# Issuing the stores of a SwiGLU kernel from GpSimd, and one gate and one product per tile in place of two

## The chip, the cores and the metric

One core of one Trainium2 chip. The metric is the time of one execution on the device in microseconds (us). The kernel before takes 936.15 us (median of 3 runs, 936.01 to 936.37). A profile records one execution; its span is some 2 us shorter than the timed run. In the views ACT is ScalarE (the gates), DVE is VectorE (the products), POOL is GpSimd and SP is SyncE; a name with q is that engine's queue of instructions. A store or load is *issued* when its engine starts it and has *landed* when its last byte is in place; a *packet* is the piece that one of the 16 DMA engines moves at a time, here a row of 64 KB (load) or 32 KB (store).

## The reference

```python
x = np.random.randn(8192, 8192).astype(np.float32)
a, b = np.split(x, 2, axis=-1)
silu_b = b / (1 + np.exp(-b))
return a * silu_b          # 8192 x 4096 float32
```

268.4 MB are read and 134.2 MB are written, with one gate and one product per output element.

## The kernel before

Two rows of x are one partition's share of a tile: 128 partitions x 16384 floats (64 KB), 32 tiles, three tile buffers. Each row is `a` (4096) and then `b` (4096). The gate works in place on `b`; the product goes to the front of the tile, from where the store takes it.

```python
R = 2; BUFS = 3                     # ntiles = 32, last = 31
def load(i, rows=None):  ...        # nc.sync.dma_start; whole tile, or one row of each pair
def swiglu(i, k, c0=0, cw=half):
    b = xt[:, k * M + half + c0 : k * M + half + c0 + cw]
    nc.scalar.activation(out=b, in_=b, func=_SILU)
    nc.vector.tensor_mul(out=xt[:, k * half + c0 : ...], in0=xt[:, k * M + c0 : ...], in1=b)
def store(i, c0=0, cw=R * half):
    (nc.scalar if i < last - 1 else nc.sync).dma_start(...)

nc.vector.memset(zt, 0.0)
nc.scalar.dma_start(out=ov[0:P, 0:128], in_=zt)     # the early zero store
for i in range(BUFS): load(i)
for i in range(last):
    for k in range(R): swiglu(i, k)
    if i == last - 1: swiglu(last, 0)
    store(i)
    ...                             # load(i + 3); the last tile in two row loads
store(last, 0, half)
...                                 # second row of the last tile in two halves, then its store
```

A load into a buffer must wait until the store of that buffer has landed. This ties everything into a ring: load, gate and product, store, next load, with three buffers going round.

Of the kernel before, what the change touches and what calls it, by code (L numbers as in the profile page):

```python
# [1 line left out]

# [4 lines left out]

_SILU = mybir.ActivationFunctionType.Silu


@with_exitstack
def kernel(
    ctx: ExitStack,
    tc: tile.TileContext,
    x: bass.AP,
    out: bass.AP,
):




    nc = tc.nc
    N, M = x.shape
    half = M // 2
    P = nc.NUM_PARTITIONS
    R = 2
    BUFS = 3

    xv = x.tensor.reshape([N // R, R * M]).ap()  # L30
    ov = out.tensor.reshape([N // R, R * half]).ap()
    ntiles = N // (P * R)
    last = ntiles - 1

    pool = ctx.enter_context(tc.tile_pool(name="sbuf", bufs=BUFS))
    tiles = {}

    def load(i, rows=None):
        if i not in tiles:
            tiles[i] = pool.tile([P, R * M], x.dtype, name="xt")  # L40
        lo, hi = (0, R) if rows is None else rows
        nc.sync.dma_start(  # L42
            out=tiles[i][:, lo * M : hi * M], in_=xv[i * P : (i + 1) * P, lo * M : hi * M]
        )

    def swiglu(i, k, c0=0, cw=half):
        xt = tiles[i]
        b = xt[:, k * M + half + c0 : k * M + half + c0 + cw]
        nc.scalar.activation(out=b, in_=b, func=_SILU)  # L49
        nc.vector.tensor_mul(  # L50
            out=xt[:, k * half + c0 : k * half + c0 + cw],
            in0=xt[:, k * M + c0 : k * M + c0 + cw],
            in1=b,
        )

    def store(i, c0=0, cw=R * half):
        (nc.scalar if i < last - 1 else nc.sync).dma_start(
            out=ov[i * P : (i + 1) * P, c0 : c0 + cw], in_=tiles[i][:, c0 : c0 + cw]
        )


    zt = ctx.enter_context(tc.tile_pool(name="zeros", bufs=1)).tile([P, 128], x.dtype, name="zt")
    ctx.enter_context(tc.manual_schedule())
    nc.vector.memset(zt, 0.0)  # L64
    nc.scalar.dma_start(out=ov[0:P, 0:128], in_=zt)

    for i in range(BUFS):
        load(i)
    for i in range(last):
        for k in range(R):  # L70
            swiglu(i, k)
        if i == last - 1:
            swiglu(last, 0)
        store(i)
        nxt = i + BUFS
        if nxt < last:
            load(nxt)
        elif nxt == last:
            load(last, (0, 1))
            load(last, (1, 2))  # L80

    store(last, 0, half)
    for c0 in range(0, half, half // 2):
        swiglu(last, 1, c0, half // 2)
    store(last, half, half)


# [1 line left out]
_INS = ['x']  # L89
_OUTS = [((8192, 4096), 'float32')]  # L90


# [23 lines left out]
```

## Time and profile before

| what | before |
|---|---|
| median time | 936.15 us |
| span of the profile | 933.9 us |
| DMA engines busy, both queues | 99.8% |
| DVE, ACT busy | 30%, 25% |
| one turn of a buffer (3 tiles) | 87.1 us |
| of it landing to store issue | 12.6 us |

First the view of DMA issues (queue, count, KB, median time from issue to landing):

```profile
out_dram<-xt ACTq DMA_DIRECT2D x30, 4096.0 KB, 40.0
...
xt<-in_x_dram SPq DMA_DIRECT2D x31, 34.2
```

A store needs 40.0 us and a load 34.2 us from issue to landing, though one tile of each passes every 29.0 us. The excess is time spent queued behind the transfer before. Then the view of windows over the middle of the span (length; busy time of DVE, ACT, POOL; clock; DMA share; GB/s):

```profile
100.00:883.00 783.00, 238.97 (x54) 192.30 (x54) 0.00 (x0) 1.00 1.00 434
```

DMA share 1.00 and 434 GB/s: the 16 engines never pause here.

### The profile page before, as it was taken

To read this page: it belongs to the slowest core of one execution; us is meant where nothing else is said; L and a number is where in the kernel's file an instruction comes from. 1 tells how busy PE (TensorE), PEld (TensorE's weight loads), DVE (VectorE), ACT (ScalarE), POOL (GpSimd) and SP (SyncE) were. 2 spreads that over 40 slices of the span, in tenths; PEclk is the share of its full clock that TensorE was granted. 3 is DMA by queue.
4 is the path that set the end of the run, shared out by engine and by line. 5 is a ranking of instruction groups with operands and counts; after the bars stand their busy time and mean duration, and the time that the engine had idled before them with its cause. 6 is when DMAs were issued, how large, how long until landed. Compare 5 with 4: busy or idle time off the path is not lost.

```text
span 933.9 us, 370 instructions
## 1 busy us (share of the span) xinstructions
DVE 283.5 (30%) x66; ACT 229.4 (25%) x66; POOL 0.2 (0%) x4
## 2 busy tenths in 40 slices
DVE  0333312333113332133321333213332133331252
ACT  0323330233312333113331133311333203332041
POOL 0000000000000000000000000000000000000000
DMA  9999999999999999999999999999999999999998
GB/s 407 422 413 460 411 431 441 449 427 420 456 408 445 431 431 441 435 422 441 448 414 436 435 451 425 429 443 414 446 427 436 436 432 425 439 451 411 441 434 383
DMA packets 9650, 402.74 MB, mean 431 GB/s; under 512 B 1072, under 2 KB 1200, under 8 KB 1200
## 3 DMA queue, kind: packets, MB, share of 16 engines
q1 hardware_dynamic: 5184, 276.83, 68.6%
q10 hardware_dynamic: 4464, 125.90, 31.2%
q14 instruction: 2, 0.02, 0.0%
HBM read 268.44 MB, written 134.28 MB: 431 GB/s over the span
## 4 chain that ended last, share of the span: by engine, by line
DMA 84%; DVE 10%; ACT 4%; DVEq 0%; issue 0%; SPq 0%; ACTq 0%
DMA out_dram<-xt 43%; DMA xt<-in_x_dram 41%; DVE xt L50 10%; ACT xt L49 4%; DVEq L111 0%; SPq L42 0%; ACTq L49 0%; DVEq L50 0%
## 5 line engine op out<-in xcount | busy, mean ns | idle before, releaser
L50 DVE TENSOR_TENSOR xt<-xt 128x4096 f32<-128x4096 f32 (+1 forms) x65 | 283.3, 4360 | 635.8 <-ACT xt L49 632.6
L49 ACT ACTIVATE xt<-xt 128x4096 f32<-128x4096 f32 (+1 forms) x65 | 228.1, 3556 | 686.5 <-DMA xt<-in_x_dram 686.5
L49 ACT ACT_TABLE_LOAD x1 | 1.3, 1283 | 1.5 <-DVE zt L64 1.5
L64 DVE MEMSET zt<- 128x128 f32 x1 | 0.2, 165 | 0.8 <-PEq L100 0.8
L100 POOL MEMSET const-bfloat16-1.0<- 128x1 bf16 x1 | 0.1, 101 | 0.0
L100 POOL MEMSET const-uint8-127<- 128x1 uint8 x1 | 0.1, 101 | 0.0
L100 POOL MEMSET const-float32-0.0<- 128x1 f32 x1 | 0.1, 98 | 0.2 <-issue 0.2
L100 POOL MEMSET const-float32-1.0<- 128x1 f32 x1 | 0.1, 98 | 0.0
## 6 DMA issues: line engine op xcount, KB each, us to landing
out_dram<-xt ACTq DMA_DIRECT2D x30, 4096.0 KB, 40.0
xt<-in_x_dram SPq DMA_DIRECT2D x2, 4096.0 KB, 26.8
out_dram<-xt SPq DMA_DIRECT2D x1, 4096.0 KB, 23.6
out_dram<-xt SPq DMA_DIRECT2D x2, 2048.0 KB, 14.5
xt<-in_x_dram SPq DMA_DIRECT2D x31, 34.2
out_dram<-zt ACTq DMA_DIRECT2D x1, 64.0 KB, 24.1
```

Of the source, the lines that this page charges most:

```text
L49: nc.scalar.activation(out=b, in_=b, func=_SILU)
L50: nc.vector.tensor_mul(out=xt[:, k * half + c0 : k * half + c0 + cw], in0=xt[:, k * M + c0 : k * M + c0 + cw], in1=b,)
L64: nc.vector.memset(zt, 0.0)
L100: nc = _bacc.Bacc("TRN2", target_bir_lowering=False, num_devices=1)
```

## The change

The intent: ACT should do only gates, GpSimd (otherwise idle) should issue the stores, and the fixed cost of half of the compute instructions should go.

```diff
+    def swiglu_tile(i):
+        rows = tiles[i].rearrange("p (k s c) -> p k s c", k=R, s=2)
+        b = rows[:, :, 1, :]
+        nc.scalar.activation(out=b, in_=b, func=_SILU)
+        nc.vector.tensor_mul(
+            out=tiles[i][:, : R * half].rearrange("p (k c) -> p k c", k=R),
+            in0=rows[:, :, 0, :], in1=b)
     def store(i, c0=0, cw=R * half):
-        (nc.scalar if i < last - 1 else nc.sync).dma_start(
+        (nc.gpsimd if i < last - 1 else nc.sync).dma_start(
     ...
     for i in range(last):
-        for k in range(R):
-            swiglu(i, k)
+        if i < BUFS:
+            for k in range(R):
+                swiglu(i, k)
+        else:
+            swiglu_tile(i)
```

More of the change, by code (lines that the diff above doesn't have):

```diff
@@ L54, in swiglu @@
         )
+    def swiglu_tile(i):
[4 more added lines that the diff above has]
+            out=tiles[i][:, : R * half].rearrange("p (k c) -> p k c", k=R),
+            in0=rows[:, :, 0, :],
+            in1=b,
+        )
     def store(i, c0=0, cw=R * half):
-        (nc.scalar if i < last - 1 else nc.sync).dma_start(
+        (nc.gpsimd if i < last - 1 else nc.sync).dma_start(
             out=ov[i * P : (i + 1) * P, c0 : c0 + cw], in_=tiles[i][:, c0 : c0 + cw]
```

## The prediction

> **What bounds the kernel now.** I read the page first (busy shares, the row of DMA shares, the queues), then the chain that ended last in order of time, then the groups of instructions by shape, the waits of the SP queue, and last the single packet records of the trace.
>
> ```profile
> span 933.9 us, 370 instructions
> DVE 283.5 (30%) x66; ACT 229.4 (25%) x66; POOL 0.2 (0%) x4
> ...
> DMA packets 9650, 402.74 MB, mean 431 GB/s; under 512 B 1072, under 2 KB 1200, under 8 KB 1200
> q1 hardware_dynamic: 5184, 276.83, 68.6%
> q10 hardware_dynamic: 4464, 125.90, 31.2%
> ```
>
> The two queues (q1 is SP with the loads and the last three stores, q10 is ACT with the other stores) add up to 99.8% of the time of all 16 DMA engines. No compute engine passes 30%. So the kernel is bound by the bytes that pass the DMA engines, loads and stores together.
>
> The packet records say how tight this is. A 64 KB load row takes 2418 ns, a 32 KB store row 1213 ns, a 16 KB row 611 ns, a 512 B row of the zero store 27 ns. These four lie on one line: about 8.5 ns a packet plus 27.2 bytes per ns. Each engine carries 8 of a tile's 128 rows, so a tile costs an engine 8 x 2418 + 8 x 1213 = 29.05 us. The windows view gives 434 GB/s in every full stretch between 100 and 883 us, and the chain shows the tiles at that same pace:
>
> ```profile
> 393.85 3.63 ACT xt L49
> 397.50 4.44 DVE xt L50
> 402.03 4.44 DVE xt L50
> 406.48 40.22 DMA out_dram<-xt
> 446.78 34.35 DMA xt<-in_x_dram
> 481.20 3.62 ACT xt L49
> ```
>
> The columns are start, length, work. From one gate (393.85) to the gate that ends one turn of the same buffer (481.20) it is 87.35 us, three tiles at 29.1 us. One turn of a buffer is load 34.4, gate and products 12.6, store 40.2. With one tile of each kind passing every 29.05 us, a load that takes 34.4 has queued about 5 us behind the load before it, and a store of 40.2 about 11 us behind the store before it. **Slack in the turn:** 87.1 - 12.6 - 2 x 29.05 = 16.4 us. So long as the compute part of the turn grows by less than this, neither queue need run empty.
>
> What is lost outside this: 32 tiles x 29.05 = 929.5 us is the floor of the packets. The first load packet starts at 1.98 us, the last data packet ends at 932.9 of 933.9. What could still be won is 933.9 - 929.5 - 2.0 - 1.0, some 1.4 us. A gain of 2% would need 917 us, below the floor of the bytes.
>
> **What the Trainium skill says.** (1) "DMA: Bandwidth & Descriptors", section "Issuing engines are not separate DMA queues": DMAs from scalar, sync or gpsimd run on the same 16 engines, and issuing from several saves only sequencer time. The trace agrees as far as it goes: two queues already share the 16 engines to 99.8%. (2) The same page, "Queues, rings and completion order": an engine takes its queues in turn, a packet of each. The trace agrees: the zero store has only 8 small packets per engine, yet lands after 24.1 us, which is about 9 turns, each behind a load packet of 2.418 us (21.8 us, and the start). (3) The same page, "SWDGE vs HWDGE vs iDMA": for a DMA from GpSimd, software on that engine writes the descriptors into rings in SBUF, and a packet is given as at most 4096 B "preferably". No GpSimd DMA is in the kernel before, so the trace can say nothing; this is the main unknown here. (4) "SBUF — State Buffer", section "SBUF: two separate sides": a 2-port DVE operation keeps GpSimd from writing descriptors, while a two-input operation conflicts only with a GpSimd operation that reads SBUF. Here DVE runs only two-input products and one memset at 0.8 us, so I expect no such stall; no trace shows it yet.
>
> **The change part by part.**
>
> ```profile
> L50 DVE TENSOR_TENSOR xt<-xt 128x4096 f32<-128x4096 f32 x63 | 278.8, 4425 | 632.3 <-ACT xt L49 629.1
> L49 ACT ACTIVATE xt<-xt 128x4096 f32<-128x4096 f32 x63 | 224.4, 3608 | 680.5 <-DMA xt<-in_x_dram 680.5
> L50 DVE TENSOR_TENSOR xt<-xt 128x2048 f32<-128x2048 f32 x2 | 4.5, 2288 | 3.5 <-ACT xt L49 3.5
> L49 ACT ACTIVATE xt<-xt 128x2048 f32<-128x2048 f32 x2 | 3.7, 1901 | 6.0 <-DMA xt<-in_x_dram 6.0
> ```
>
> After the bar: busy us in total, mean ns, idle before. Two lengths of each give a line. ACT: (3608 - 1901) / 2048 = 0.834 ns an element, 194 ns fixed; 8192 elements: 7.02 us. DVE: (4425 - 2288) / 2048 = 1.043 ns, 151 ns fixed; 8192: 8.70 us.
>
> *One gate and one product for tiles 3 to 30.* 28 tiles x 2 instructions fall to 28 each; 56 instructions fewer in all. ACT busy falls by 28 x 0.194 = 5.4 us, DVE by 28 x 0.151 = 4.2 us. None of it is on the path, as both idle before every tile for about 20 us. What gets longer is the time from landing to product: before, gate of row 0, then two products, 12.6 us; after, 7.02 + 8.70 + 0.03 = 15.75 us, because the product no longer overlaps the second gate. **Plus 3.15 us per tile**, taken from the 16.4 us of slack.
>
> *Stores from GpSimd, 30 of 32 tiles.* ACT loses 30 issues of 0.34 us and its wait for the product, worth nothing as its next gate is 20 us off. GpSimd has to make 128 rows' descriptors for each. I have no duration of that in this trace; what matters is that 16.4 - 3.15 = 13 us would have to be used up before the DMA could run out of work. It comes right after a product, when DVE next works some 13 us later. Bytes and rows stay; if rows remain packets of 32 KB, the DMA time is 0 different. In turn the loads and stores keep sharing 2 to 1.
>
> *First tiles and end.* Tiles 0 to 2 are by rows as before. The first store has to go through a queue that was not used yet, since the zero store stays on ACT: in the trace of before, the first real store, issued at 35.40, had its first packet at about 39.98, with load packets slowed to 3.3 us around it. A late first store costs nothing while the loads of tiles 1 and 2 (to 74.5) are in the queue. At the end:
>
> ```profile
> 890.75 8.95 DVE L50 TENSOR_TENSOR xt<-xt 128x4096 f32<-128x4096 f32 x2 [20.02 <-ACT xt L49]
> 899.73 20.74 SPq L57 DMA_DIRECT2D out_dram<-xt  x3
> 904.04 3.62 ACT L49 ACTIVATE xt<-xt 128x4096 f32<-128x4096 f32 x1 [9.81 <-DMA xt<-in_x_dram]
> 907.69 4.42 DVE L50 TENSOR_TENSOR xt<-xt 128x4096 f32<-128x4096 f32 x1 [7.99 <-ACT xt L49]
> 913.67 3.71 ACT L49 ACTIVATE xt<-xt 128x2048 f32<-128x2048 f32 x2 [6.02 <-DMA xt<-in_x_dram]
> ```
>
> Tile 30's store is on SP behind the loads of tile 31, which land at 904.0 and 913.67. Its issue moves from 899.7 to about 902.9, still 11 us before its turn. DVE is free at 902.9, before row 0's product at 907.69. After 913.67 the SP queue still has 4.19 + 2.10 + 2.10 MB of stores, 19.3 us at 434 GB/s, far longer than the last half row's compute of 6.4 us. So the end is set by bytes and is not moved. Sum: 0 from compute, 0 from the loop, and I allow +0.5 us for the extra queue's start and end: **936.6 us**.
>
> **The rivals.** (A) *Smaller packets.* If software descriptors cut a 32 KB row into 4 KB, each engine gets 2048 store packets in place of 256; 1792 x 8.5 ns = 15 us, so 951 us (+1.6%). At 2 KB it is 3840 x 8.5 = 33 us, 969 us (+3.5%). Also each piece would wait for a 64 KB load in turn, so that stores crawl until the loads dry up. For it: the skill's preferred packet. Against it: the same trace moves 64 KB rows as single packets from SP and ACT, and the page gives the 4096 B as a preference. I give it 7%, half of that past 2%. (B) *A wait that replaces one.* If a GpSimd store becomes visible late, by over 13 us a tile, the load queue runs empty between a store's landing and the next load; each microsecond beyond it costs up to a third of one per tile, as three buffers share a turn: 5 us too much would be 5/3 x 28 = 47 us. Against it: 128 rows are few. 2%. (C) *One of the 16 engines is slowed* by the fetching of descriptors, and every tile waits for it: 50 ns on each of 256 store packets is 13 us, 949 us. Against it: two descriptors of some bytes beside 32 KB. 4%. (D) *Gain from an ACT that no longer waits, and fewer instructions.* ACT waits 686.5 us for loads, so nothing is gained; at best part of the 1.4 us of loss comes back: 934.7 us.
>
> **Range and chances.** The main case (some 87%) is 935 to 939, with runs of before within 0.4 us. A cost of a new queue of a few us at start or end, and part of A and C, set the upper end: 934.8 to 941. Faster by 2% is excluded by the floor of bytes: 0.01. Slower by 2% (over 954.9) needs A at 2 KB or less, B, or a strong C: 0.05. Same: 0.94.
>
> **What would show it.** Right: a software queue with about 3840 packets of 32 KB, none added under 8 KB beyond the semaphores; DMA share 9 in all slices, 434 GB/s from 100 to 883; ACT x28 at 7.02 us, DVE x28 at 8.70 us; load plus store in one turn down by some 3 to 5 us, to about 70, with the turn still 87. Wrong: many more packets, slices at 8 or less, a period over 29.1 us, or a stretch of more than 1 us at an end without packets.

## The result, and the profile after

| | before | after |
|---|---|---|
| median (6 runs each, range) | 935.98 (935.76 to 936.37) | 936.66 (936.42 to 937.12) |
| ratio | | 1.0007, 95% interval 0.9994 to 1.002 |

A ratio here is the mean time of one kernel's runs over that of the other's in the same rounds, so it is not quite the ratio of the medians quoted. All runs in this document are at clock 1.00. The six runs of each do not overlap, so some 0.7 us are likely to be real, far under 2%.

The page of the kernel after:

```profile
span 934.7 us, 319 instructions
DVE 279.0 (30%) x38; ACT 226.8 (24%) x38; POOL 16.3 (2%) x34
...
DMA packets 9652, 402.76 MB, mean 431 GB/s; under 512 B 1072, under 2 KB 1200, under 8 KB 1200
q1 hardware_dynamic: 5184, 276.83, 68.5%
q0 software_dynamic: 4320, 125.83, 31.2%
q10 hardware_dynamic: 144, 0.07, 0.0%
```

The store bytes moved from q10 to a new queue q0 of kind software_dynamic. Of its 4320 packets 480 are semaphores (30 stores x 16 engines) and 3840 are rows; the lower counts of small packets are the same as before, so a row is still one packet. The packet records give 1213 ns on average, as on ACT's queue (2 of the 3840 took over 1250).

The chain of the kernel after, at the same place as in the prediction (start, length, work):

```profile
394.00 7.04 ACT xt L60
401.06 8.70 DVE xt L61
409.76 0.28 issue
410.05 36.75 DMA out_dram<-xt
446.80 0.02 SPq L42
446.85 34.03 DMA xt<-in_x_dram
480.99 7.04 ACT xt L60
```

From landing to store issue it is now 16.05 us (394.00 to 410.05) in place of 12.63. The store lands after 36.75 us in place of 40.22. The load is unchanged, and the turn is 87.0 us again: **the 3.4 us that compute took longer came wholly out of the time that stores spend queued**. The view of DMA issues and the same window say so for all tiles:

```profile
out_dram<-xt POOLq DMA_DIRECT2D x30, 4096.0 KB, 36.7
...
xt<-in_x_dram SPq DMA_DIRECT2D x31, 34.0
```
```profile
100.00:883.00 783.00, 234.70 (x27) 189.79 (x27) 14.35 (x27) 1.00 1.00 434
```

The groups of the kernel after (count, busy us, mean ns, idle before):

```profile
L61 DVE TENSOR_TENSOR xt<-xt 128x8192 f32<-128x8192 f32 x28 | 243.4, 8693 | 573.4 <-ACT xt L60 573.4
L60 ACT ACTIVATE xt<-xt 128x8192 f32<-128x8192 f32 x28 | 196.8, 7029 | 616.7 <-DMA xt<-in_x_dram 616.7
...
L68 POOL DMA_DIRECT2D out_dram<-xt x30 | 16.1, 536 | 858.5 <-DVE xt L61 773.8
```

7029 and 8693 ns against 7.02 and 8.70 us predicted. A store costs GpSimd 0.53 us, after 0.28 us from the product's end; on ACT the issue took 0.34 us.

The end of the kernel after, by the timeline:

```profile
894.20 8.69 DVE L61 TENSOR_TENSOR xt<-xt 128x8192 f32<-128x8192 f32 x1 [19.99 <-ACT xt L60]
902.92 17.66 SPq L68 DMA_DIRECT2D out_dram<-xt  x3
904.14 3.62 ACT L49 ACTIVATE xt<-xt 128x4096 f32<-128x4096 f32 x1 [9.97 <-DMA xt<-in_x_dram]
907.79 4.42 DVE L50 TENSOR_TENSOR xt<-xt 128x4096 f32<-128x4096 f32 x1 [4.89 <-ACT xt L49]
913.78 3.71 ACT L49 ACTIVATE xt<-xt 128x2048 f32<-128x2048 f32 x2 [6.03 <-DMA xt<-in_x_dram]
```

Tile 30's store is issued at 902.92 in place of 899.73, and the last loads land at 904.1 and 913.8 as before. The late issue lost nothing.

Where are the 0.8 us between the spans? From the first data packet to the end of the last it is 930.95 us before and 930.94 after. The difference lies behind the last packet: the span ends 1.26 us after it before, and 2.02 us after it now. SP's waits for transfers at the program's end show the reason in part, before and then after (total, times, longest):

```profile
SPq L111 <- DMA out_dram<-xt: 12.5, 1, 12.5
```
```profile
SPq L125 <- DMA out_dram<-xt: 12.3, 3, 4.8
```

SP now checks eight wait instructions there in place of four, about 60 ns each where nothing is left to wait for; and the records show 0.42 us between the starts of two of its drain instructions that are 0.06 us apart in the kernel before; the second took 0.13 us in place of 0.01.

### The profile page after: what moved, and what is told of

It is laid out like the page before. It is cut to its first block, busy times and chain, and to the rows that moved or that the text cites. A ratio compares the mean times of both kernels' runs of the same rounds, so it can differ in the third digit from the quotient of the medians.

```text
span 934.7 us, 319 instructions
## 1 busy us (share of the span) xinstructions
DVE 279.0 (30%) x38; ACT 226.8 (24%) x38; POOL 16.3 (2%) x34
## 3 DMA queue, kind: packets, MB, share of 16 engines
q0 software_dynamic: 4320, 125.83, 31.2%
## 4 chain that ended last, share of the span: by engine, by line
DMA 81%; DVE 10%; ACT 7%; issue 0%; DVEq 0%; SPq 0%; ACTq 0%
DMA xt<-in_x_dram 41%; DMA out_dram<-xt 40%; DVE xt L61 8%; ACT xt L60 7%; DVE xt L50 1%; ACT xt L49 1%; DVEq L125 0%; SPq L42 0%; ACTq L60 0%; DVEq L50 0%
## 5 line engine op out<-in xcount | busy, mean ns | idle before, releaser
L61 DVE TENSOR_TENSOR xt<-xt 128x8192 f32<-128x8192 f32 x28 | 243.4, 8693 | 573.4 <-ACT xt L60 573.4
L60 ACT ACTIVATE xt<-xt 128x8192 f32<-128x8192 f32 x28 | 196.8, 7029 | 616.7 <-DMA xt<-in_x_dram 616.7
L50 DVE TENSOR_TENSOR xt<-xt 128x4096 f32<-128x4096 f32 (+1 forms) x9 | 35.5, 3950 | 67.0 <-ACT xt L49 66.6
L49 ACT ACTIVATE xt<-xt 128x4096 f32<-128x4096 f32 (+1 forms) x9 | 28.7, 3230 | 72.5 <-DMA xt<-in_x_dram 72.5
L68 POOL DMA_DIRECT2D out_dram<-xt x30 | 16.1, 536 | 858.5 <-DVE xt L61 773.8
## 6 DMA issues: line engine op xcount, KB each, us to landing
out_dram<-xt POOLq DMA_DIRECT2D x30, 4096.0 KB, 36.7
```

The lines of the kernel that those rows point to most:

```text
L50: nc.vector.tensor_mul(out=xt[:, k * half + c0 : k * half + c0 + cw], in0=xt[:, k * M + c0 : k * M + c0 + cw], in1=b,)
L61: nc.vector.tensor_mul(out=tiles[i][:, : R * half].rearrange("p (k c) -> p k c", k=R), in0=rows[:, :, 0, :], in1=b,)
L68: (nc.gpsimd if i < last - 1 else nc.sync).dma_start(out=ov[i * P : (i + 1) * P, c0 : c0 + cw], in_=tiles[i][:, c0 : c0 + cw])
```

## The experiments

Theory: the DMA engines' bytes set the time, and what the change adds (3.4 us per tile) fits into the queueing time of the ring; the 0.7 us are an end cost of the new queue. Rivals: the two halves of the change cancel (one gains, the other loses); smaller packets; descriptors blocked by DVE; a slack that is smaller or larger than worked out. Twelve kernels ran, all with correct results. "Base" is the kernel before on the same chip in the same rounds.

### Halves of the change: e1, e2, e3

e1: `if i < BUFS:` becomes `if True:` (by rows throughout, stores from GpSimd).

> All 31 tiles by rows as in the kernel before, stores of tiles 0 to 29 from GpSimd as in the kernel after. Theory 1 (the 0.7 us that the change costs is a fixed end cost of stores from a software queue: more semaphores for the program's end to wait for and clear): 936.7 us, last data packet at 932.9 us of the span as in both kernels, span end some 1.8 us after it. Theory 2 (the 0.7 us comes from the longer time from landing to product): 936.0. Either way landing to product is 12.6 us again, the store's landing some 40 us, and the turn of a buffer 87.1 us.

e2: `nc.gpsimd` becomes `nc.scalar` again (one gate and product, stores from ACT).

> One gate and one product per tile from the fourth tile on, stores from ACT as in the kernel before. Theory 1 (fixed end cost of the software queue): 936.0 us, span end about 1.0 us after the last data packet. Theory 2 (longer landing to product): 936.7. Landing to product 15.75 us, store about 37 us, turn 87.1 us.

e3: in the kernel before, `nc.gpsimd if i == 15 else nc.scalar if i < last - 1 else nc.sync`.

> The kernel before with the store of tile 15 alone from GpSimd. Theory 1a (the end cost comes with the mere presence of a software queue): 936.5 to 936.7 us. Theory 1b (it grows with the number of semaphores that the software stores use, eight with 30 stores, one with one): 936.0 to 936.2, the span ending about 1.1 us after the last data packet. The DMA rate is 434 GB/s in both.

| run (5 runs, base 935.81) | median us | ratio (95%) | last data packet to end of span | SP instructions |
|---|---|---|---|---|
| e1 rows, GpSimd | 936.68 | 1.0009 (0.9996 to 1.0021) | 1.91 | 83 |
| e2 whole tile, ACT | 935.81 | 1.0000 (0.9986 to 1.0013) | 1.26 | 78 |
| e3 one store from GpSimd | 936.03 | 1.0002 (0.999 to 1.0015) | 1.31 | 80 |

The intervals don't part the theories, as each holds 1, though all runs of e1 (936.40 to 937.14) lie above all of the base (to 936.31) and of e2 (to 936.11). The records are of a finer grain: the longer end goes with GpSimd's stores (e1) and not with the longer compute (e2), and a single such store costs 0.04 us, so mere presence isn't it (1a falls). (The ends of 1.8, 1.0 and 1.1 us in these expectations rest on packet times that were 0.24 us late; see the point on the floor of the bytes below.) e2 also shows the ring at work without GpSimd: its stores land after 34.7 us and its loads after 36.3, so there the queueing has shifted from stores to loads, at the same total.

The later runs correct this reading. In e11 and e12 below, with all 30 stores from GpSimd too but 108 instructions on SP, the end is 1.49 and 1.56 us: there SP's drains are 0.06 us apart. So of the 0.76 us some 0.2 to 0.3 are the additional semaphores, and most of the rest is a pause of SP of some 0.4 us that comes with 83 or 84 instructions on its queue (the kernel after, e1, e9, and e10, where it stands before the first drain) and not with 78 to 80 or 108. The pause may be a fetch of instructions: in the four kernels that have it, an 8 KB packet of the kind "instruction" starts 0.63 to 0.66 us behind the pause's end, and in e11 and e12 none starts after 803 us. But it comes behind the pause and not in it, so no run settles that.

### How much longer may compute take: e4, e5, e6, e7, e11, e12

The prediction put the limit from landing to store at 12.6 + 16.4 = 29.0 us. These runs lengthen that time in the kernel after by operations that leave the result as it is. e4 and e5, one and two of:

```diff
+        o = tiles[i][:, : R * half]
+        nc.vector.tensor_max(out=o, in0=o, in1=o)
```

> The kernel after with one more product-sized DVE operation per tile behind the product (the maximum of the result with itself, which leaves it as it is): 8.7 us more from landing to store, 24.7 us in all. The prediction's slack (16.4 us over the 12.6 of before, that is up to 29.0 us) is not used up: 936.7 us, with the store's landing down from 36.7 to about 29 us. Rival (work-conserving DMA): 936.7 as well.

> Two more such DVE operations per tile: 33.4 us from landing to store, 4.4 us beyond the slack of the prediction. Prediction's theory (each microsecond beyond costs a third of one per tile): 4.4 / 3 x 28 = 41 us, so 978 us. Rival (the DMA engines lose nothing while either the load queue or the store queue has work; the true limit is a turn of 87.1 less a load alone, 19.3, less a store alone, 9.7, that is 58 us): 937 us, with the load's landing falling toward 25 us or the store's toward 20.

e6 and e7 add, beside the two, two and three copies on ACT between gate and product:

```diff
+        for _ in range(2):   # e7: 3
+            nc.scalar.copy(out=rows[:, :, 0, :], in_=rows[:, :, 0, :])
```

> Two more DVE operations and two more ACT operations (copies in place of the first factor) per tile: 17.4 + 14.1 us more, some 47.5 us from landing to store. Prediction's theory: (47.5 - 29.0) / 3 x 28 = 173 us more, 1109 us. Rival (limit 58 us): 937 to 945 us.

> A third ACT copy: some 54.5 us from landing to store, ACT 28.1 of 29 us busy per tile. Prediction's theory: (54.5 - 29.0) / 3 x 28 = 238 us more, 1175 us. Rival (limit 58 us less the time from a landing to the next packet, twice some 2 us in a turn, so 54): just at the limit, 940 to 975 us.

After these four, e11 and e12 looked for the limit, with the maximum over 4096 and 6144 of the 8192 columns.

> The kernel after with one more DVE operation over half of each result (128x4096, 4.42 us) behind the product: some 20.5 us from landing to store. The slack as predicted (13 us left after the change) was refuted by 8.7 us more, which cost 29 us; this run asks how much of it is real. Theory C (a load issued into a queue that has run dry starts with no packets for some 2 us and with packets of 3.1 to 3.2 us in place of 2.42, so that the queues must overlap by several us, and the 12.7 us of overlap that the trace of the kernel after shows, 34.0 + 36.7 - 2 x 29.0, are needed but for 3 to 4): at the knee, 937 to 945 us, with slow load packets in the middle of the trace. Rival (the knee lies near the 8.7 us): 936.7 us and at most a handful of slow load packets.

> The kernel after with one more DVE operation over three quarters of each result (128x6144, 6.56 us): some 22.6 us from landing to store. 4.4 us more cost nothing (936.07), 8.7 us cost 29. Theory C' (no load queue restart until the overlap of successive loads and stores, 12.7 us in the kernel after, has shrunk to about 4 to 5): 12.7 - 6.6 = 6.1 us of overlap are left, so 936 to 938 us. Rival (the cost sets in with the first microsecond past 4.4 and grows by 29 / 4.3 us): 936 + (6.56 - 4.4) x 6.8 = 951 us.

| run | landing to store issue, us | median us | base | ratio (95%) | data packets per engine, us | span |
|---|---|---|---|---|---|---|
| after | 16.05 | 936.66 | 935.98 | 1.0007 | 931.8 | 934.7 |
| e11 | 20.8 | 936.07 | 936.00 | 0.9998 (0.9981 to 1.0014) | 931.9 | 934.7 |
| e12 | 22.9 | 937.49 | 936.15 | 1.0009 (0.9992 to 1.0025) | 933.9 | 936.3 |
| e4 | 25.0 | 965.67 | 936.25 | 1.0320 (1.0282 to 1.0357) | 954.2 | 968.6 |
| e5 | 33.8 | 1000.33 | 936.25 | 1.0690 (1.0672 to 1.0708) | 963.1 | 996.5 |
| e6 | 47.7 | 1053.05 | 936.25 | 1.1245 (1.1228 to 1.1262) | 977.6 | 1051.6 |
| e7 | 54.8 | 1067.12 | 936.25 | 1.1400 (1.1383 to 1.1417) | 978.3 | 1067.4 |

**Both theories that stood for e4 to e7 missed.** The prediction's slack gave no cost for e4 and 978, 1109 and 1175 us for the others; the work-conserving rival gave some 937 almost up to e7. The true limit lies between 22.9 and 25.0 us, earlier than the prediction had it, and beyond it the cost is neither zero nor a third of each microsecond.

The windows view of e4 shows what happens at the limit (same columns as above):

```profile
461.00:463.00 2.00, 2.00 (x1) 0.00 (x0) 0.00 (x0) 1.00 0.72 311
463.00:464.00 1.00, 0.84 (x1) 0.00 (x0) 0.00 (x0) 1.00 0.01 0
464.00:465.00 1.00, 0.00 (x0) 0.00 (x0) 0.53 (x1) 1.00 0.15 66
465.00:466.00 1.00, 0.00 (x0) 0.00 (x0) 0.00 (x0) 1.00 1.82 492
```
```profile
464.39 0.53 POOL L70 DMA_DIRECT2D out_dram<-xt  x1 [31.91 <-DVE xt L67]
```

(A packet is counted where it starts, hence 1.82.) At 463 a load and a store run out together, while the third buffer is still in compute. By 464 thirteen of the 16 engines have posted the end of the load and have nothing; three are still at its last packets. GpSimd issues the next store at 464.4, SP the next load at 464.74, once the store has landed. The store's packets start at 465.48, those of the load only at 467.42, 2.7 us after its issue, and the load's first packet on nearly every engine takes 2.9 to 3.4 us in place of 2.42. The load's packets had to wait for the store's first packets, which ran from 465.5 to 467.5 and were slow themselves (1.8 to 2.0 us in place of 1.21). So a dry moment costs twice: the pause, and slow packets behind it. In the table the data packets of an engine sum to 22 us more in e4 than after (load packets over 2.45 us: 473 in place of 39), and the pauses, what the span holds beside them, grow from 3.0 to 14.4 us. The first load packets of the kernel before, at the start of its span, are slow in the same way (2.8 to 3.3 us). Why packets are slow after a pause is not shown.

The last run that is still "same" shows how much queueing must be left, by its view of DMA issues:

```profile
out_dram<-xt POOLq DMA_DIRECT2D x30, 4096.0 KB, 31.4
...
xt<-in_x_dram SPq DMA_DIRECT2D x31, 32.6
```

In e12 stores land after 31.4 us and loads after 32.6, with 29.0 per tile: 2.4 and 3.6 us in the queue, some 6 in sum. It is not wholly free: three of its four runs (937.49 to 938.05) lie above all of its base (to 936.62), and it has 94 slow load packets where the kernel after has 39 and e11 41. So e12 stands at the edge. In e4 87.1 - 25.0 - 58.1 = 4 us would have been left at the full rate, and it did not hold. So between 4 and 6 us of the 16.4 are needed, where the prediction let them fall to zero; the usable slack is about 10.3 us (e12, at the edge) and under 12.4 (e4, not free), of which the change uses 3.4. That the need comes from the engines being apart at a landing (2 to 4 us in the middle of e12), so that some run dry before the last one lets the next transfer start, fits in size, but is argued and not tested by itself. Of the expectations, e12's first theory held (936 to 938) and its rival (951) fell; e11's theory C, which had put the limit there, fell, and its rival held.

Further out, the cost per tile (28 tiles) is 1.0 us in e4, 2.3 in e5, 4.2 in e6 and 4.7 in e7: more than a third of the first microseconds past the limit (e4), less of the later ones. Slow packets grow to some 46 us in e6 and stay there in e7; the pauses go on growing, to 86 us beyond those of the kernel after. No formula of mine gives these sizes.

### Smaller packets: e8

```diff
+        step = 1024 if i < last - 1 else cw
+        for c in range(c0, c0 + cw, step):
+            ...dma_start(out=ov[..., c : c + step], in_=tiles[i][:, c : c + step])
```

> The kernel after with each GpSimd store cut into eight stores of 1024 columns, so that the store packets are 4 KB: eight times as many, 30720 in place of 3840. Prediction's rival A, by its sum: 30 tiles x 8 rows x 7 more packets per engine x 8.5 ns = 14.3 us more of DMA time, and 7 x 30 more semaphore packets of 9 ns (1.9 us): about 952 to 953 us. If a 4 KB packet also waits for a 64 KB load packet in turn, stores take far longer to land (64 packets x 2.4 us = 155 us if loads never dried up) and the loads run dry between; a DMA that has work in either queue then loses nothing beyond the 16 us; with gaps at each dry end it is 960 to 1000 us.

962.74 us (base 936.17), ratio 1.0291 (1.0274 to 1.0308). The page:

```profile
DMA packets 39894, 402.79 MB, mean 419 GB/s; under 512 B 4432, under 2 KB 4560, under 8 KB 35280
...
q0 software_dynamic: 34560, 125.84, 32.3%
```

A 4 KB packet takes 159 ns, as 8.5 ns + 4096 / 27.2 gives. The store packets of an engine sum to 307.8 us in place of 291.1, and 1.9 us of semaphores come to it: 18.5 us where 16.2 were expected, so rival A's sum was nearly right as far as it went. But the run lost 26 us, since load packets were slowed as well (mean 2471 ns in place of 2425, 553 slow ones), 11 us per engine. A piece, an eighth of a store, landed after 29.2 us in the median, and the eight of one tile were issued over some 17 us (415.6 to 432.6 us, for one), so a whole store needed some 46 us, far from the 155 of the expectation. The run is no pure test: GpSimd also waited 422.8 us in all for the landings of earlier pieces before it could issue later ones, which one store per tile doesn't do. With that reservation, rows cut to 4 KB cost 2.9% where rival A's sum gave 1.6%; the change itself keeps its rows whole.

### DVE copies beside the descriptors: e9

```diff
+            for _ in range(8):
+                nc.vector.tensor_copy(out=w[:, 1664:3328], in_=w[:, 0:1664])
```

> The kernel after with eight copies of 128x1664 fp32 on DVE right behind each product, beside which GpSimd makes the store's descriptors. If such copies keep GpSimd from writing descriptors, its store issue grows from 0.53 us to several us (at most the copies' whole 8 to 14 us); by the slack the time stays at 936.7 us either way. If they don't, issue stays 0.53 us and the time 936.7 us.

937.15 us (base 936.17), ratio 1.001 (0.9995 to 1.0024). The timeline, at the same place:

```profile
401.30 8.69 DVE L61 TENSOR_TENSOR xt<-xt 128x8192 f32<-128x8192 f32 x1 [11.93 <-ACT xt L60]
409.91 8.45 DVE L89 COPY w<-w 128x1664 f32<-128x1664 f32 x8
410.29 0.76 POOL L68 DMA_DIRECT2D out_dram<-xt  x1 [28.23 <-DVE xt L61]
```

A copy takes 1026 ns for 1664 elements, 0.62 ns each, against 1.04 for a product, so its elements go through faster; in which mode DVE ran it the record doesn't say. GpSimd's issue beside it grew from 0.53 to 0.76 us, so neither expectation held. The trace shows more than the length: in all 27 stores beside copies the issue began 0.38 us after the first copy did and ended 0.12 us behind that copy's end, while the next copy, 0.03 us behind the first, was running. That is what a block until the end of the copy under way would look like; as every issue met its copy at the same moment, a slowing of another kind that ends there by chance is not excluded. The copies after it did not hold the store up: by the packet records each of these stores had its first packet 0.7 to 2.2 us before the last copy ended. (That stores land after 36.7 us as in the kernel after says little, as they queue behind the store before for longer than that.) So what these copies cost a store is 0.23 us; one long copy was not tried.

e9 is a control for e4 as well: it adds 8.2 us of DVE time per tile beside the store's path at no cost, where e4 adds 8.7 in the path and loses 29 us. So e4 pays for the delay and not for DVE's work.

### Two buffers: e10

`BUFS = 2`.

> The kernel after with two tile buffers in place of three (tiles 0 and 1 by rows). Turn at full rate 58.1 us for two tiles. Prediction's theory (a load and a store must each always be queued): slack 58.1 - 58.1 - 16 is 16 us short, 16 / 2 x 30 = 240 us more, 1177 us. Rival (work-conserving): the engines are idle only between a store's landing and the next load's first packet, while the other buffer computes, 2 to 4 us per tile: 990 to 1060 us.

1048.05 us (base 936.17), ratio 1.1196 (1.1179 to 1.1213), inside the range of the rival and far from the 1177 of the prediction's formula. An engine's data packets sum to 980.2 us (48 more than after) in a span of 1047.0. The other 64 us (1047.0 - 980.2 - 3.0) are pauses, 2.1 per tile for 30 tiles, as the rival had it; the slow packets behind each pause come on top and were in neither sum.

## Why the prediction was right, point by point

- **Time**: 936.6 predicted, 936.66 measured, in the range, verdict "same". That it agrees to 0.1 us is partly luck: the allowance of 0.5 us was a guess, 0.18 too low, on a base of 936.15 that six runs put at 935.98.
- **The floor of the bytes** held: rows stayed packets of 2418 and 1213 ns, and the data took 930.94 us from first to last packet. The three packet times quoted in the prediction (1.98, 39.98 and 932.9 us) are all 0.24 us late, as I set the origin of the records wrongly; they are 1.74, 39.74 and 932.7, and the 3.0 us lost at the two ends stay.
- **One gate, one product**: 7.03 and 8.69 us, landing to product 15.75 as worked out. ACT's busy time fell by 2.6 us (229.4 to 226.8) and not by 5.4, as two gates in a row took 7.12 us together and not twice 3.61; DVE's fell by 4.5 where 4.2 were expected. Neither is on the path. e2 shows that this half alone moves the time by nothing.
- **Stores from GpSimd**: the duration left open is 0.53 us plus 0.28 before it. DVE's next product begins some 20 us after a product's end (438.75 to 459.06, for one), not 13, which makes the case for no collision only stronger. e1 shows that this half alone costs the end cost and nothing else.
- **The end is set by bytes**: confirmed to 0.1 us on both row loads.
- **+0.5 us for the extra queue**: 0.68 measured by the medians, all of it behind the last packet; part is the queue's semaphores, part a pause of SP that had not been foreseen and doesn't come with GpSimd's stores as such (e11, e12).
- **Rivals**: A (smaller packets) and C (a slowed engine) are refuted by 3840 packets of 1213 ns on average; e8 shows what A would have cost, and that the sum given for it left out the slowed loads. B is refuted by an issue that begins 0.28 us after the product and stores that land after 36.7 us. D found nothing to gain.
- **What was wrong without harm**: the step from 16.4 us of slack to "So long as the compute part of the turn grows by less than this, neither queue need run empty", and with it rival B's "each microsecond beyond it costs up to a third". The step that failed is the end of the slack: the queues may not shrink until they are empty. The limit is some 10 us, not 16.4, as 4 to 6 us of queueing must be left; 12.4 us of growth lose 29 us. The change used 3.4 us, so the conclusion stood, with less room than I believed.

## What to carry to other kernels

In this kernel, whose DMA engines never pause, work moved between compute engines or issuing queues gained nothing; in one like it, look at issue-to-landing against the period per tile to see how much delay is free. Don't count that queueing time as free down to zero: here the last 4 to 6 us of 16 were needed, and once they were touched the time rose by 3%. Keep rows as large packets: cut to 4 KB they cost 2.9% here (e8).

## What the Trainium skill lacked or had wrong

- "DMA: Bandwidth & Descriptors", SWDGE vs HWDGE vs iDMA: it gives a packet as at most 4096 B preferably. Here GpSimd's stores ran as 32 KB packets, 3840 of them at 1213 ns, the same as from ACT. It has no time for a GpSimd issue of a large plain store either: 0.53 us, 0.28 us after the product's end; ACT's took 0.34.
- No page that I read has the slow packets behind a pause of the DMA engines: 1.8 to 2.0 us for 32 KB in place of 1.21, and 2.9 to 3.4 for 64 KB in place of 2.42 (e4). Nor how much queueing such a ring of buffers needs: 4 to 6 us here.
- No page that I read has what a second kind of DMA queue costs at the program's end: 0.2 to 0.3 us of waits and clears for its semaphores, and a pause of some 0.4 us more in some programs.

Nothing was found wrong. "SBUF — State Buffer", SBUF: two separate sides, has GpSimd locked out while DVE runs a 2-port operation, an fp32 copy among them; e9 fits that, with an issue of 0.76 in place of 0.53 us that ended 0.12 us behind the end of the copy under way. The two-operand products ran beside no issue, so they remain untested.
